# Layer 1 of a two-layer trunk: the loads of a recurrence unit in a task of their own, the exponential taken in place, and a shorter step of the recurrence's clock

## The chip, the cores and the metric

The kernel runs on one core of one Trainium2 chip. The metric is the device time of one execution in microseconds (us); lower is better. The times before are the median of three executions, 2402.3 us (2398.12 to 2408.5). One further execution was profiled.

## The reference, cut to what matters

A trunk of two layers works on x of 512 tokens by 2048 channels. Layer 0 is softmax attention with forget gates. Layer 1 is RWKV-7 time mixing, and the change lies there. Its heads have 64 channels each:

```python
w_log = -jax.nn.softplus(-(w0 + jnp.tanh(xw @ w1) @ w2)) - 0.5
decay = jnp.exp(-jnp.exp(w_log))
def step(S, inp):                       # one token, for each of 32 heads
    r_t, w_t, k_t, v_t, a_t, b_t = inp
    sa = einsum('bhvk,bhk->bhv', S, a_t)
    S = S * w_t + sa[..., None] * b_t + v_t[..., None] * k_t
    y_t = einsum('bhvk,bhk->bhv', S, r_t)
    return S, y_t
y = groupnorm(y) + sum(rh * kh * r_k) * vh
out = (y * silu(z)) @ w_out
```

## The kernel before, in words

**How the work is laid out.** Every large product (q, k, v, z, r and the two output projections) is a matrix of 16 by 16 blocks of 128 by 128. A block times 128 x 512 activations takes three TensorE matmuls, since weights and activations are split into a high and a low part (`mm3`, lines 253 to 258). These matmuls write the tiles `pj`. For every four blocks of weights there is one load of 256 KB (`raw`), one copy on ScalarE that makes the high part (`whi`) and one subtraction on VectorE that makes the low part (`wlo`).

**The recurrence.** Layer 1's recurrence is done in chunks of 64 tokens. There are four head groups of eight heads, and each has eight chunks, two to a unit: 16 units, numbered 0 to 15 here, and 32 chunks. For each unit `stage` (lines 1477 to 1527) loads three things with DMAs that SyncE (SP) issues: `rt` (256 KB), `bk` (four loads of 128 KB) and `prk` (256 KB, the running sum of the log decay, from the DRAM tensor `ipd`). Then ScalarE makes `eI`, the exponential of that sum; VectorE multiplies `rt` by `eI`, and GpSimd copies the chunk's total decay to `dec`. VectorE writes into `prk` the product of `rt`, a vector and `bk` in eight steps (tile `prk` again, lines 1499 to 1505). Then each chunk's loads `L`, `QP` and `SV` are issued, and a task `products` is started for each chunk. `products` makes the chunk's small matrices through two PSUM banks `S` (lines 1529 to 1567; ScalarE reads them into `L` and `GP`) and ends with the copy `tok`. `recur` (lines 1590 to 1644) carries the state `SV` from chunk to chunk in three steps: small matmuls into `x`, copies by VectorE into `xs` and `SV`, and again. `normed` normalizes a unit's output and stores it to `ypd`; `gated` loads it back (`yp`), multiplies by the gate (`z`), and from there the operands of the last projection are made (`gd`, `hp`, `hi`, `lo`).

**What sets the order.** All tasks are generators run by a small planner (`Flow`, lines 108 to 129). Its clock advances with the matmuls as they are issued, by 512/2400 us for a `pj` matmul. A task that yields d is resumed d planner microseconds later. `backbone` issues the `pj` matmuls one after another and lets due tasks put their instructions between them. So the order of each engine's instructions is fixed when the program is built; on the chip each engine works its own list in order and waits on semaphores for the others. SP's list is kept free for the scheduler to arrange within the dependencies.

**Numbers that matter here.** `STW` = 5 is the planner time between the load of `prk` and the exponential. `HOP` = 3.9 is the grid on which the recurrence's steps fall (`hop`, lines 1585 to 1588), three steps to a chunk. At most four chunks are staged and not yet consumed (`free["chunk"]`), and `rt`, `bk`, `prk` and `eI` have two buffers each.

Of the kernel before, what the change touches and what calls it, by code (L numbers as in the profile page):

```python
# [9 lines left out]
F = mybir.dt.float32  # L10
R = mybir.dt.float32r
AF = mybir.ActivationFunctionType
# [5 lines left out]
P = 128  # L18
# [6 lines left out]
C = 64  # L25
NCH = T // C
NJ, UC = 4, 2
# [104 lines left out]
def body(ctx, tc, a, out, dbg=None, stop=0):  # L132
# [1339 lines left out]

    HS = (slice(0, 64), slice(64, 128))
    OS = (slice(64, 128), slice(0, 64))
    QP, GP, svs, staged = [], [], {}, {}

    def stage(q, g, u):

        rt = q.tile([P, NJ, UC, C], F, tag="rt", name="rt", bufs=2)
        sp.dma_start(rt.rearrange("p j c t -> p j (c t)"), rTd[g][:, u])  # L1480
        bk = q.tile([P, NJ, UC, 2, C], F, tag="bk", name="bk", bufs=2)
        yield 1
        for i in range(2):
            for h in range(2):
                sp.dma_start(bk.rearrange("p j c i t -> p (j c) i t")[HS[h], :, i, :],
                             bkd[g][HS[h], u, i ^ h].rearrange("p j (c t) -> p (j c) t", c=UC))
            yield 0.6
        yield from take("prk")
        prk = q.tile([P, NJ, UC, C], F, tag="prk", name="prk", bufs=2)
        sp.dma_start(prk.rearrange("p j c t -> p j (c t)"), ipd[g][:, u])  # L1490
        yield STW
        eI = q.tile([P, NJ, UC, C], F, tag="eI", name="eI", bufs=2)
        act.activation(eI, prk, AF.Exp, scale=-EDEC)
        yield 1
        dec = q.tile([P, NJ, UC], F, tag="dec", name="dec", bufs=3)
        pool.tensor_copy(dec, eI[:, :, :, C - 1])
        dve.tensor_tensor(out=rt, in0=rt, in1=eI, op=OP.mult)
        yield 1
        for j in range(NJ):
            for h in range(2):  # L1500
                s = HS[h]
                dve.scalar_tensor_tensor(out=prk[s, j], in0=rt[s, j],
                                         scalar=vecs[s, V_RK, NJ * g + j:NJ * g + j + 1],
                                         in1=bk[s, j, :, 1 - h, :], op0=OP.mult, op1=OP.mult)
            yield 0.6
        while any(NJ * g + i not in vd for i in range(NJ)):
            yield 0.2
        for c in range(UC):
            yield from take("chunk")
            m = NCH * g + UC * u + c  # L1510
            L, SV = ([q.tile([P, NJ] + w, F, tag=f"{m}{h}", name=f"{m}{h}", bufs=4)
                      for h in range(2)] for m, w in (("L", [2, C]), ("SV", [C])))
# [12 lines left out]
            fl.start(fl.t + STW, products(q, m, c, L, SV, qp, bk, eI, dec))  # L1525
            yield 2
        fl.start(fl.t + 2, bonus(q, g, u, prk))

    def products(q, m, c, L, SV, qp, bk, eI, dec):

        gp = GP[m % 4]
        yield from hop()
        ns = yield from need2("S")
        gs = [bank("S") for _ in ns]
        for j in range(NJ):
            for h in range(2):
                s = HS[h]
                pe.matmul(gs[h][:, j * P:(j + 1) * P],
                          bk[s, j, c].rearrange("p a t -> p (a t)"),
                          L[h][s, j].rearrange("p a t -> p (a t)"), start=True, stop=True)  # L1540
        yield 0.9
        for h in range(2):
            s, t = HS[h], OS[h]
            g3 = gs[h].rearrange("p (j n) -> p j n", j=NJ)
            act.activation(L[h][t].rearrange("p j a t -> p j (a t)"), g3[t], AF.Copy)
            act.activation(gp[h][s], g3[s, :, C:], AF.Copy)
            read("S", ns[h])
            pool.affine_select(out=L[h][t], in_=L[h][t], pattern=[[0, NJ], [1, 2], [1, C]],
                               compare_op=OP.is_ge, fill=0.0, base=-1,
                               channel_multiplier=-1)  # L1550
            pool.affine_select(out=gp[h][s], in_=gp[h][s], pattern=[[0, NJ], [1, C]],
                               compare_op=OP.is_ge, fill=0.0, base=0, channel_multiplier=-1)
            yield 0.9
        pool.tensor_tensor(out=bk[:, :, c], in0=bk[:, :, c],
                           in1=eI[:, :, c, C - 1:C].unsqueeze(2).broadcast_to([P, NJ, 2, C]),
                           op=OP.mult)
        yield 4
        n = yield from need("S")
        tr = bank("S")
        for j in range(NJ):  # L1560
            pe.transpose(tr[:, j * P:(j + 1) * P], bk[:, j, c].rearrange("p a t -> p (a t)"),
                         ident)
        yield 0.6
        tok = q.tile([P, NJ, 2, C], F, tag="tok", name="tok", bufs=4)
        act.activation(tok.rearrange("p j h t -> p (j h t)"), tr, AF.Copy)
        read("S", n)
        staged[m] = SV, L, qp, gp, dec, tok

    def bonus(q, g, u, prk):
        vv = q.tile([P, T], F, tag="vv", name="vv", bufs=1)  # L1570
# [181 lines left out]

    STW = 5
    DG, DINV = (3,), 32
    HOP = 3.9
    INV, KEY = 54, 9.8

    def side(q):
        for j, o in enumerate(ks):
            fl.start(0, keep(j, o))  # L1760
        for k in range(KT):
            fl.start(fl.t, lora_k(q, k))
            yield 5.2
        while len(lb) < 4:
            yield 0.2
        yield 0.5
        pools.close()
        q = pools.enter_context(tc.tile_pool(name="uq", bufs=2, reuse_waits="tile"))
        for n in range(3):
            fl.start(fl.t, lora_w(q, 0, n))  # L1770
        rmask = q.tile([P, NCH, C], F, name="rmask", bufs=1)
        pool.memset(rmask, 1.0)
        pool.memset(rmask[:, :, 0:1], 0.0)
        rms.append(rmask)
        lora_act(q)
# [12 lines left out]
        eIs.append(kp.tile([P, NCH, C + 1], F, name="eI"))  # L1788
        for i in range(5):
            qts.append(kp.tile([P, NCH, C], F, name=f"qt{i}"))  # L1790
            for r in (32, 96):
                pool.memset(qts[i][r:r + 32, :, 0:32], 0.0)
        pool.memset(eIs[0][:, :, 0:1], 1.0)
        for j in range(KT):
            if "v" in dbg:
                print("keys", j, fl.t, len(ends))
            fl.start(fl.t, keys(kp, j))
            fl.start(fl.t + 5, mixz(kp, j))
            yield KEY
        while len(qd) < KT or len(premixed) < 3 * KT:  # L1800
            yield 0.2
        yield 3
        pools.close()
        rk = pools.enter_context(tc.tile_pool(name="rk", bufs=1, reuse_waits="tile"))
        for i in range(4):
            QP.append([rk.tile([P, NJ, C], F, name=f"QP{i}{h}") for h in range(2)])
            GP.append([rk.tile([P, NJ, C], F, name=f"GP{i}{h}") for h in range(2)])
            for h in range(2):
                pool.memset(QP[i][h][OS[h]], 0.0)
                pool.memset(GP[i][h][OS[h]], 0.0)  # L1810
        def stages():
            for n in range(NG * NU):
                g, u = divmod(n, NU)
                while any(NJ * g + i not in rd for i in range(NJ)):
                    yield 0.2
                yield from stage(rk, g, u)

        fl.start(fl.t, stages())
        fl.start(fl.t, recur(rk))

# [40 lines left out]
```

## Time and profile before

| | |
|---|---|
| median of three runs | 2402.3 us (2398.12 to 2408.5) |
| the profiled execution's own time | 2401.73 us |
| span from its first to its last instruction | 2399.9 us |
| TensorE (PE) busy | 2302.2 us, 96% |
| VectorE (DVE), ScalarE (ACT), GpSimd (POOL) busy | 1605.2, 1256.5, 694.4 us |
| layer 1's recurrence: first load of a unit to last `ypd` store issued | 1698.4 to 2197.7 us of the span |

A row of the timeline gives the start in us of the span, how long it took, the engine, the operation, what it wrote and read, and in square brackets how long the engine was idle before it and what ended that. SPq is the queue of SP, whose rows are issues of DMAs; the landing comes later. All instructions go through a helper on line 90, so they are told apart by their tiles. The row of an engine's waits names who waited, for whom, and gives the total, the count and the longest. In the table of windows the columns are the stretch and its length, then busy time and count for PE, PE's weight load, DVE, ACT and POOL, then the granted TensorE clock, the DMA engines' busy share and GB/s.

### The profile page before, as it was taken

The page shows a single profiled execution, that of the slowest core. Times are in us where ns is not written, and L with a number is a line of the kernel's source. Part 1 is how long each engine was busy: PE and PEld are TensorE (multiplying, and loading weights), DVE is VectorE, ACT ScalarE, POOL GpSimd, SP SyncE. Part 2 cuts the span into 40 slices and gives each one's busy share as a digit, 9 for nine tenths or more (in the row PEclk, how much of TensorE's full clock was granted, in tenths as well). Part 3 has the DMA queues.
Part 4 walks back from the last instruction along what each step waited for, and adds up shares of the span by engine and source line. Part 5 has one row for each costly group of instructions (what it writes and reads, how often), then busy time and mean ns, then how long its engine had stood idle before and what let it go on. Part 6 is the DMA issues. An engine that isn't in the chain of part 4 may idle for free. (4 is left out here: it accounts for less than half of the span.)

```text
span 2399.9 us, 39413 instructions
## 1 busy us (share of the span) xinstructions
PE 2302.2 (96%) x13626; PEld 1807.3 (75%) x13626; DVE 1605.2 (67%) x2850; ACT 1256.5 (52%) x2300; POOL 694.4 (29%) x1114
## 2 busy tenths in 40 slices
PE   6999999999999999998999898899999899999999
PEld 4787777877778778886777676677777677777787
DVE  6886778888888635336797567666476776755322
ACT  4435655555565545225646777763345556665221
POOL 0002333442424210110141208771245535450000
PEclk8999999999999999999999999899999999999999
DMA  8864466766666346445756999886867766544543
GB/s 307 328 227 156 128 211 217 222 213 213 205 224 220 114 161 225 142 141 157 223 179 198 308 263 277 256 252 187 233 187 195 219 174 194 167 132 154 161 137 97
DMA packets 388152, 480.23 MB, mean 200 GB/s; under 512 B 146032, under 2 KB 217840, under 8 KB 384112
## 3 DMA queue, kind: packets, MB, share of 16 engines
q1 hardware_dynamic: 386288, 475.08, 63.7%
q0 software_dynamic: 1664, 2.63, 0.3%
q8 instruction: 108, 1.77, 0.3%
q14 instruction: 92, 0.75, 0.1%
HBM read 381.63 MB, written 95.95 MB: 199 GB/s over the span
## 5 line engine op out<-in xcount | busy, mean ns | idle before, releaser
L90 PE MATMUL pj<-hi,whi 128*128 128x512 f32 x2416 | 987.4, 409 | 11.0 <-ACT hi L90 8.2
L90 PE MATMUL pj<-hi,wlo 128*128 128x512 f32 x2416 | 959.4, 397 | 10.1 <-DVE wlo L90 10.0
L90 PE MATMUL pj<-lo,whi 128*128 128x512 f32 x2416 | 959.9, 397 | 0.0
L90 DVE TENSOR_TENSOR wlo<-raw,whi 128x512 fp32r<-128x512 f32 (+2 forms) x628 | 473.4, 761 | 255.1 <-ACT whi L90 252.4
L90 ACT ACTIVATE whi<-raw 128x512 fp32r<-128x512 f32 (+2 forms) x628 | 393.9, 634 | 399.0 <-PE pj L90 215.1
L90 PEld LDWEIGHTS pj<-hi,whi 128*128 128x128 f32 x2416 | 459.5, 190 | 116.8 <-ACT hi L90 9.2
L90 PEld LDWEIGHTS pj<-lo,whi 128*128 128x128 f32 x2416 | 458.3, 190 | 108.4 <-DVE lo L90 0.7
L90 PEld LDWEIGHTS pj<-hi,wlo 128*128 128x128 f32 x2416 | 459.9, 190 | 105.2 <-DVE wlo L90 13.4
L90 DVE CUSTOM_DVE_ANT_0 wm<-wm,cb 128x1024 f32<-128x1024 f32 x128 | 155.8, 1217 | 0.3
L90 POOL TENSOR_SCALAR SV<-SV,dec 64x64 f32<-64x64 f32 x224 | 94.2, 442 | 103.9 <-DVE SV L90 69.7
L90 ACT ACTIVATE pr<-Sm,mx 128x128 f32<-128x128 f32 (+3 forms) x128 | 71.5, 559 | 76.8 <-POOL mx L90 76.3
L90 POOL TENSOR_SCALAR pr<-pr,rc 128x128 f32<-128x128 f32 (+3 forms) x128 | 100.8, 788 | 26.0 <-DVE rc L90 23.6
L90 POOL TENSOR_SCALAR mx<-mx 128x1 f32<-128x1 f32 x128 | 59.9, 468 | 143.2 <-DVE mx L90 98.0
L90 DVE CUSTOM_DVE_ANT_0 Sm<-S,cmask 128x128 f32<-128x128 f32 (+3 forms) x128 | 62.3, 487 | 42.5 <-PE S L90 41.8
L90 POOL TENSOR_TENSOR lt<-lane 128x30 f32<-128x30 f32 (+14 forms) x90 | 64.2, 713 | 86.4 <-DMA lane<-mld 79.6
L90 POOL TENSOR_TENSOR bk<-bk,eI 128x512 f32<-128x512 f32 x32 | 36.6, 1142 | 110.3 <-PE S L90 64.0
L90 POOL TENSOR_TENSOR lane<-lane,lt 128x30 f32<-128x30 f32 (+14 forms) x90 | 64.0, 711 | 7.0
L90 PE MATMUL S<-k,q 128*128 128x128 f32 (+7 forms) x256 | 61.9, 323 | 0.0
L90 POOL TENSOR_TENSOR acc<-acc,sq 128x512 f32<-128x512 f32 x14 | 18.1, 1296 | 149.4 <-ACT sq L90 128.2
L90 ACT ACTIVATE pT<-tr 128x512 f32<-128x512 f32 x64 | 31.0, 485 | 54.4 <-PE tr L90 54.4
L90 DVE SCALAR_TENSOR_TENSOR hp<-pj,gate,hp 128x512 f32<-128x512 f32 x16 | 12.0, 751 | 68.0 <-PE pj L90 68.0
L90 PE MATMUL tr<-ident,pr 128*128 128x128 f32 x320 | 56.0, 273 | 1.5 <-DVE pT L90 1.3
(325 smaller groups left out, 3284.0 us busy)
## 6 DMA issues: line engine op xcount, KB each, us to landing
wm<-in_wmodT SPq DMA_DIRECT2D x132, 512.0 KB, 4.4
raw<-in_wz SPq DMA_DIRECT2D x128, 256.0 KB, 3.7
raw<-in_wo SPq DMA_DIRECT2D x128, 256.0 KB, 3.6
raw<-in_wv SPq DMA_DIRECT2D x124, 256.0 KB, 3.9
wm<-in_wmodT SPq DMA_DIRECT2D x30, 1024.0 KB, 6.4
raw<-in_wk SPq DMA_DIRECT2D x96, 256.0 KB, 3.7
raw<-in_wr SPq DMA_DIRECT2D x64, 256.0 KB, 5.0
raw<-in_wq SPq DMA_DIRECT2D x56, 256.0 KB, 3.5
```

Of the source, the lines that this page charges most:

```text
L90: self.last = f(*a, **k)
```

## The change

The loads move out of `stage` into a new task, `arrive`. A second generator, `arrivals`, runs it for the units in order, as soon as the group's `rt` is ready (as before) and, for units 2 and on, once the last chunk of the unit before the one before has been made (`made`, set by `products` after `tok`). `stages` starts 9 planner us later than before and waits until a unit's loads have all been issued (`got`). The running sum is no longer loaded into `prk` but into `eI`, and the exponential is taken in place; `prk` only receives the product. The load of the sum moves from behind the loads of `bk` to before them, and `bk`'s four loads are a planner microsecond apart each. The fixed `yield STW` ahead of the exponential is gone (`STW` stays in use ahead of `products`). `HOP` is 3.75 in place of 3.9.

```diff
-    def stage(q, g, u):
+    def arrive(q, g, u, got):
         rt = q.tile([P, NJ, UC, C], F, tag="rt", name="rt", bufs=2)
         sp.dma_start(rt.rearrange("p j c t -> p j (c t)"), rTd[g][:, u])
+        yield 1
+        eI = q.tile([P, NJ, UC, C], F, tag="eI", name="eI", bufs=2)
+        sp.dma_start(eI.rearrange("p j c t -> p j (c t)"), ipd[g][:, u])
+        yield 1
         bk = q.tile([P, NJ, UC, 2, C], F, tag="bk", name="bk", bufs=2)
-        yield 1
         for i in range(2):
             for h in range(2):
                 sp.dma_start(bk.rearrange("p j c i t -> p (j c) i t")[HS[h], :, i, :],
                              bkd[g][HS[h], u, i ^ h].rearrange("p j (c t) -> p (j c) t", c=UC))
-            yield 0.6
+                yield 1
+        got[NU * g + u] = rt, eI, bk
+
+    def stage(q, g, u, rt, eI, bk):
         yield from take("prk")
         prk = q.tile([P, NJ, UC, C], F, tag="prk", name="prk", bufs=2)
-        sp.dma_start(prk.rearrange("p j c t -> p j (c t)"), ipd[g][:, u])
-        yield STW
-        eI = q.tile([P, NJ, UC, C], F, tag="eI", name="eI", bufs=2)
-        act.activation(eI, prk, AF.Exp, scale=-EDEC)
+        act.activation(eI, eI, AF.Exp, scale=-EDEC)
...
         staged[m] = SV, L, qp, gp, dec, tok
+        made.add(m)
...
-    HOP = 3.9
+    HOP = 3.75
...
+        got = {}
+
+        def arrivals():
             for n in range(NG * NU):
                 g, u = divmod(n, NU)
-                while any(NJ * g + i not in rd for i in range(NJ)):
+                while any(NJ * g + i not in rd for i in range(NJ)) or \
+                        n > 1 and UC * (n - 1) - 1 not in made:
                     yield 0.2
-                yield from stage(rk, g, u)
+                yield from arrive(rk, g, u, got)
 
+        def stages():
+            yield 9
+            for n in range(NG * NU):
+                while n not in got:
+                    yield 0.2
+                yield from stage(rk, *divmod(n, NU), *got.pop(n))
+
+        fl.start(fl.t, arrivals())
         fl.start(fl.t, stages())
```

What the change makes of the order of instructions shows at three places. First SP's list at unit 10 (third head group), from the load of `rt` on. The number behind a name tells one buffer's use from the next; `x2` are two like rows. Before:

```order
L90 DMA rt_20570<-rTd_125 128x512
L90 DMA SV0_20528<-vtd_127 64x256
L90 DMA SV1_20529<-vtd_127 64x256
L90 DMA bk_20572<-bkd_117 64x8x64 x2
L90 DMA vv_20616<-vvd_126 128x512
L90 DMA bk_20572<-bkd_117 64x8x64 x2
L90 DMA yp_20626<-ypd_128 128x4x128
L90 DMA prk_20633<-ipd_122 128x512
L90 DMA raw_20635<-in_wz1 128x512
```

And the same place now:

```order
L90 DMA rt_20473<-rTd_125 128x512
L90 DMA eI_20481<-ipd_122 128x512
L90 DMA bk_20486<-bkd_117 64x8x64 x2
L90 DMA L0_20513<-atd_116 64x4x64
L90 DMA QP30_17180<-qtd_118 64x4x64
L90 DMA SV0_20515<-vtd_127 64x256
L90 DMA L1_20514<-atd_116 64x4x64
L90 DMA QP31_17181<-qtd_118 64x4x64
L90 DMA SV1_20516<-vtd_127 64x256
L90 DMA bk_20486<-bkd_117 64x8x64
L90 DMA raw_20543<-in_wz1 128x512
L90 DMA bk_20486<-bkd_117 64x8x64
```

The running sum's load stands right behind `rt`'s, where eight other loads stood between them, and the last two loads of `bk` now stand behind six loads of another unit's chunk.

Next DVE's list at the same unit, from the last weight part ahead of the unit on. `rt<-rt,eI` is the first use of the exponential, `prk<-rt,vecs,bk` the first use of `bk`, and `SV`, `xs` and `x` are the recurrence. Before:

```order
L90 TENSOR_TENSOR wlo_20701<-raw_20635,whi_20700 128x512
L90 TENSOR_TENSOR rt_20570<-rt_20570,eI_20703 128x512
L90 SCALAR_TENSOR_TENSOR prk_20633<-rt_20570,vecs_63,bk_20572 64x128 x2
L90 TENSOR_TENSOR mlo_20746<-prk_20296,mhi_20745 128x512
L90 SCALAR_TENSOR_TENSOR prk_20633<-rt_20570,vecs_63,bk_20572 64x128 x4
L90 COPY xs_20784<-x_20775 128x256
L90 SCALAR_TENSOR_TENSOR prk_20633<-rt_20570,vecs_63,bk_20572 64x128 x2
```

And now:

```order
L90 TENSOR_TENSOR mlo_20549<-ys_20537,mhi_20548 128x512
L90 TENSOR_TENSOR rt_20473<-rt_20473,eI_20481 128x512
L90 SCALAR_TENSOR_TENSOR prk_20588<-rt_20473,vecs_63,bk_20486 64x128 x4
L90 COPY SV0_19950<-x_20559 64x256
L90 COPY SV1_19951<-x_20559 64x256
L90 SCALAR_TENSOR_TENSOR prk_20588<-rt_20473,vecs_63,bk_20486 64x128 x4
L90 TENSOR_TENSOR mlo_20636<-sq_20603,mhi_20635 128x512
```

The uses of the exponential and of `bk` follow each other as before; two copies of the recurrence's state now stand between the two halves of `bk`'s use.

Last DVE's list near the end of layer 1, where `z<-z,yp` applies the gate to tiles 12 and 13, `wlo` are weights, and `lo<-hp,hi` are operands of the last projection. Before:

```order
L90 TENSOR_TENSOR lo_23527<-hp_23452,hi_23526 128x512
L90 TENSOR_TENSOR z_23381<-z_23381,yp_23471 128x512
L90 TENSOR_TENSOR z_23272<-z_23272,yp_23473 128x512
L90 TENSOR_TENSOR lo_23541<-hp_23468,hi_23540 128x512
L90 TENSOR_TENSOR lo_23558<-hp_23485,hi_23557 128x512
L90 TENSOR_TENSOR wlo_23555<-raw_23496,whi_23554 128x512
L90 TENSOR_TENSOR lo_23578<-hp_23502,hi_23577 128x512
L90 TENSOR_TENSOR wlo_23570<-raw_23508,whi_23569 128x512
```

And now:

```order
L90 TENSOR_TENSOR z_23310<-z_23310,yp_23352 128x512
L90 TENSOR_TENSOR wlo_23400<-raw_23363,whi_23399 128x512
L90 TENSOR_TENSOR wlo_23432<-raw_23381,whi_23431 128x512
L90 TENSOR_TENSOR lo_23435<-hp_23406,hi_23434 128x512
L90 TENSOR_TENSOR lo_23453<-hp_23413,hi_23452 128x512
L90 TENSOR_TENSOR z_23402<-z_23402,yp_23404 128x512
L90 TENSOR_TENSOR lo_23469<-hp_23415,hi_23468 128x512
L90 TENSOR_TENSOR wlo_23466<-raw_23408,whi_23465 128x512
```

The two gatings stood one behind the other, seven operands deep into the last projection's list; now the first stands ahead of the first of these operands, and the second two operands behind it.

More of the change, by code (lines that the diff above doesn't have):

```diff
@@ L1474, in body @@
     OS = (slice(64, 128), slice(0, 64))
-    QP, GP, svs, staged = [], [], {}, {}
-    def stage(q, g, u):
+    QP, GP, svs, staged, made = [], [], {}, {}, set()
+    def arrive(q, g, u, got):
         rt = q.tile([P, NJ, UC, C], F, tag="rt", name="rt", bufs=2)
         sp.dma_start(rt.rearrange("p j c t -> p j (c t)"), rTd[g][:, u])
+        yield 1
+        eI = q.tile([P, NJ, UC, C], F, tag="eI", name="eI", bufs=2)
+        sp.dma_start(eI.rearrange("p j c t -> p j (c t)"), ipd[g][:, u])
+        yield 1
         bk = q.tile([P, NJ, UC, 2, C], F, tag="bk", name="bk", bufs=2)
-        yield 1
         for i in range(2):
@@ L1810, in side @@
                 pool.memset(GP[i][h][OS[h]], 0.0)
-        def stages():
+        got = {}
+        def arrivals():
             for n in range(NG * NU):
                 g, u = divmod(n, NU)
-                while any(NJ * g + i not in rd for i in range(NJ)):
+                while any(NJ * g + i not in rd for i in range(NJ)) or \
+                        n > 1 and UC * (n - 1) - 1 not in made:
                     yield 0.2
-                yield from stage(rk, g, u)
+                yield from arrive(rk, g, u, got)
[6 more added lines that the diff above has]
+        fl.start(fl.t, arrivals())
         fl.start(fl.t, stages())
```

## The prediction

> **What bounds the kernel now.** The page comes first, for what is busy and for how long.
>
> ```profile
> span 2399.9 us, 39413 instructions
> PE 2302.2 (96%) x13626; PEld 1807.3 (75%) x13626; DVE 1605.2 (67%) x2850; ACT 1256.5 (52%) x2300; POOL 694.4 (29%) x1114
> ```
>
> PE is the bound, and the change neither adds nor removes a matmul. So time can only come from the stretches in which PE stands still or has half its clock, and only behind the first instruction that moves, the loads of unit 0 at 1698 us. The windows of 100 us from there say how much there is (the first column after the length is PE's busy time; the granted clock stands behind POOL's count).
>
> ```profile
> 1700.00:1800.00 100.00, 96.26 (x804) 76.14 (x804) 64.84 (x133) 43.14 (x80) 44.91 (x93) 0.98 0.77 205
> 1800.00:1900.00 100.00, 98.56 (x1000) 77.40 (x998) 76.92 (x169) 53.71 (x100) 51.23 (x94) 1.00 0.71 197
> 1900.00:2000.00 100.00, 89.86 (x892) 69.22 (x893) 71.46 (x146) 57.22 (x100) 43.78 (x88) 0.97 0.69 192
> 2000.00:2100.00 100.00, 98.86 (x970) 77.49 (x969) 70.00 (x157) 65.55 (x106) 47.67 (x90) 1.00 0.64 181
> 2100.00:2200.00 100.00, 99.44 (x880) 78.39 (x877) 55.65 (x122) 59.52 (x96) 32.08 (x61) 1.00 0.38 117
> 2200.00:2300.00 100.00, 97.01 (x414) 77.23 (x413) 38.64 (x60) 30.39 (x49) 0.00 (x0) 1.00 0.58 176
> ```
>
> PE's idle time is 3.74 + 1.44 + 10.14 + 1.14 + 0.56 + 2.99 = 20.0 us: 0.8% of the kernel, and half of it in one window. That is the ceiling of any gain, but for the clock. PE's waits in this stretch and the timeline say what the idle time is made of.
>
> ```profile
> PE S L90 <- ACT GP L90: 9.7, 5, 5.3
> PE S L90 <- ACT mhi L90: 3.5, 1, 3.5
> PE pj L90 <- DVE wlo L90: 2.9, 3, 1.5
> ...
> 1907.04 0.42 SPq L90 DMA_DIRECT2D rt<-rTd  x1
> 1911.91 0.89 SPq L90 DMA_DIRECT2D prk<-ipd  x1
> 1917.31 0.63 ACT L90 ACTIVATE eI<-prk 128x512 f32<-128x512 f32 x1 [4.09 <-DMA prk<-ipd]
> 1918.96 0.38 ACT L90 ACTIVATE GP<-S 64x256 f32<-64x256 f32 x1
> 1919.39 0.79 PE L90 MATMUL S<-mhi,blkr 128*128 128x512 f32 x1 [5.28 <-ACT GP L90]
> ```
>
> This is unit 8, the largest stall. SP issued the load of the running sum 4.87 us behind that of `rt`, since `bk`'s loads and others stood between. ACT reached the exponential first and waited 4.09 us for the load. The reads of the PSUM banks (`L`, `GP`) stood behind it in ACT's list, PE needed such a bank, and so PE stood still for 5.28 us. The same chain shows once more in small, at unit 5:
>
> ```profile
> 1830.10 0.63 ACT L90 ACTIVATE eI<-prk 128x512 f32<-128x512 f32 x1 [1.60 <-DMA prk<-ipd]
> 1831.67 0.50 PE L90 MATMUL S<-mhi,blkr 128*128 128x512 f32 x1 [1.00 <-ACT GP L90]
> ```
>
> Two of 16 units paid on PE. The large stall also cost clock: the windows of 20 us show a granted clock of 0.93 behind it.
>
> ```profile
> 1900.00:1920.00 20.00, 12.80 (x142) 9.64 (x142) 13.02 (x22) 11.62 (x22) 13.60 (x29) 0.90 0.90 257
> 1920.00:1940.00 20.00, 19.03 (x185) 14.72 (x184) 18.80 (x41) 10.93 (x20) 6.32 (x12) 0.93 0.61 161
> 1940.00:1960.00 20.00, 19.56 (x178) 15.24 (x179) 15.74 (x35) 9.40 (x17) 6.89 (x17) 1.00 0.56 149
> ```
>
> In 1920 to 1940 that is 20 x 0.07 = 1.4 us of matmul time lost. The Trainium skill ("TensorE: Matmul & The Clock Gate", the section on what is actually happening) has the clock halved once PE was idle for a window of some 3.4 us, and restored after a busy window as long: by it the price would be an estimated 1.7 us. By that rule the sum below would be 0.3 us larger; the row decides.
>
> The other big stall, at 1737, has another cause: ACT waited for a weight load. The clock behind it was 0.95, 20 x 0.05 = 1 us.
>
> ```profile
> 1735.81 0.63 ACT L90 ACTIVATE whi<-raw 128x512 fp32r<-128x512 f32 x1 [3.08 <-DMA raw<-in_wv]
> 1737.01 0.49 PE L90 MATMUL S<-mhi,blkr 128*128 128x512 f32 x1 [3.46 <-ACT mhi L90]
> ...
> 1740.00:1760.00 20.00, 20.00 (x200) 16.05 (x197) 11.01 (x24) 8.79 (x17) 9.21 (x17) 0.95 0.72 195
> ```
>
> **The exponential's load comes sooner.** By the planner's yields nothing is gained: from the load of `eI` to `got` there are still five yields of 1, as STW was 5. The rest of "one unit ahead" is small, because `arrivals` must wait until the unit before last is made. What does gain is SP's list. Between the loads of `rt` and of the sum stood 4 to 8 other issues at units 0 to 10 before; now at most 4 do, and mostly none or one. For unit 8, with its gap of 4.87 us, one is left. What a load takes from issue to landing, and what an issue takes of SP, stands in the rows of the tiles `prk` and `bk` (the latter in 1690 to 2200):
>
> ```profile
> L90 SPq DMA_DIRECT2D prk<-ipd x16: 326/680/1747, 1702.2 to 2089.8; - x16
> DMA to landing us min/median/max: 2.6/4.7/5.9
> ...
> L90 SPq DMA_DIRECT2D bk<-bkd x64: 573/626/1296, 1698.9 to 2103.9; - x64
> DMA to landing us min/median/max: 2.6/4.4/6.3
> ```
>
> Planner time is shorter than the chip's. A row near the end of the chain of waits gives PE's pace without disturbance:
>
> ```profile
> 2226.59 169.46 PE pj L90 x728
> ```
>
> A `pj` matmul takes 169.46 / 728 = 0.233 us where the planner books 0.213, a ratio of 1.09. Five planner microseconds are 5.5 us, more than the median landing of 4.7 and less than the longest, 5.9: at most 0.4 us of wait is left. So I take off unit 8's 5.28 + 1.4 and unit 5's 1.00: **-7.7 us**. Bounds: 0, if the loads slip as before, and -7.7.
>
> **The shorter HOP and the end of the recurrence.** In PE's list the first chunk's `x` stands behind 5304 `pj` matmuls (5295 before), the last chunk's behind 6267 (6321 before). The recurrence ends 54 x 0.233 = 12.6 us of filler earlier. That by itself is no time, as PE's filler only changes places. It pays where the end is late today, at the last projection:
>
> ```profile
> 2208.99 0.69 DVE L90 TENSOR_TENSOR z<-z,yp 128x512 f32<-128x512 f32 x1 [3.85 <-DMA yp<-ypd]
> 2211.55 0.50 PE L90 MATMUL pj<-hi,wlo 128*128 128x512 f32 x1 [0.77 <-DVE wlo L90]
> 2218.96 0.50 PE L90 MATMUL pj<-hi,wlo 128*128 128x512 f32 x1 [1.55 <-DVE wlo L90]
> 2225.24 0.69 DVE L90 TENSOR_TENSOR z<-z,yp 128x512 f32<-128x512 f32 x1 [2.54 <-DMA yp<-ypd]
> 2226.59 0.50 PE L90 MATMUL pj<-hi,wlo 128*128 128x512 f32 x1 [0.57 <-DVE wlo L90]
> ```
>
> Tiles 12 and 13 waited in DVE's list, with weights behind them; their operands came late. Both gatings now stand some 12 us earlier against the filler, and 0.77 + 1.55 go: **-2.3 us** (bounds 0 and -2.9). Tiles 14 and 15 stand where they stood, since they follow their own matmuls; the 0.57 stays. A tighter recurrence costs nothing on PE, I think: its dependent steps in PE's list are about as far apart at the least as before, 2.4 us of other matmuls counted at the pace above.
>
> **`bk` comes later, and this costs.** Before, the last load of `bk` was issued 0.6 + 5 + 1 + 1 = 7.6 planner us ahead of its first use; now at least 1 + 1 + 1 = 3, or 3.3 us on the chip, where landing takes 4.4 in the median. That alone is 1.1 us of wait on DVE for each unit. SP's list is worse: in ten of the 16 units the last load of `bk` stands 10 to 15 issues behind that of `eI` (12.8 in the mean, the others' chunk loads between), where at units 0 to 12 it stood ahead of the sum's load. Twelve or thirteen issues are 12.8 x 0.626 = 8.0 us, and with 4.4 to land 12.4; the first use is due 7 planner us behind `eI`'s load at the least, 7.6 us. The wait is then up to 4.8 us. I take half, 2.4 us at ten units, 24 us of DVE, since stages that wait for a chunk leave more lead and SP often runs ahead.
>
> What PE pays of it: a wait of DVE of 3.85 us let PE stand for 0.77 (rows above), a fifth; ACT's wait of 4.09 cost 5.28, 1.3 times. Behind `bk`'s use stand weights, covered by the parts made ahead, and the state copies of the recurrence, which PE wants only a step later. I take the fifth, as the row of the same engine: **+4.8 us**. Bounds: 0, and 10 x 4.8 x 1.3 = +62, which I hold for far out. The Trainium skill ("DMA: Bandwidth & Descriptors", the rules for kernel authors) advises to issue a DMA early and wait for it late; by that rule the edit to `bk` is the wrong way round. The page's fit for the GpSimd path (anatomy of one DMA, 2.0 us and the bytes at 436 GB/s) would have 128 KB land in an estimated 2.3 us, and the sum without this cost; the trace's 4.4 decides.
>
> **The rest.** The exponential in place, `prk` without a load and the wait for `made` add no instruction that computes. SP may wait for a buffer: `eI` and `bk` are now loaded soon after the unit before last is made. Weights queue behind that on SP, three buffers deep. I count nothing for it. The stalls of 3.46 at 1737 and the remainder I leave as they are: other orders make other stalls of this size.
>
> **Sum.** -7.7 - 2.3 + 4.8 = -5.2. The profiled execution took 2401.73 us, span and 1.8 us around it; that gives 2396.5. The median of the runs is 0.6 higher: **2397 us**.
>
> **Rivals.** Half a per cent, 12 us, is about what a measurement of this kernel can tell from no change.
>
> - *`bk` waits land on PE.* With 48 us of DVE waits (ten times 4.8) and the state copies `SV` right behind them in DVE's list, PE pays more than a fifth. For it: a whole step of the recurrence is only 3.75 planner us, 4.1 us, and copies held for 4.8 exceed it. Against it: most steps have slack from DVE's own speed. It decides from a share of 22 / 48 = 0.46 on; at 0.6 it gives 2402.3 - 10 + 29 = 2421.
> - *Even pace.* In PE's list the two `products` of a unit stood mostly 9 to 15 `pj` apart; from unit 3 on they stand 24 to 39 apart. If this also clears half of the remaining 20.0 - 5.28 - 1.00 - 2.32 = 11.4 us of stalls, and `bk` costs nothing: 2402.3 - 10.0 - 5.7 = 2386.6. With all of it and the clock lost behind the stall at 1737, some 1 us, 2380 is the floor.
> - *It isn't ahead.* If the lead of 5.5 us is eaten by SP, ACT waits as before, and only the end gains: 2402.3 - 2.3 = 2400.
>
> **Chances.** Forecast 0.45, not ahead 0.15 (both within 0.5%), even pace 0.28, `bk` on PE 0.12. So faster by over 0.5% 0.28, within 0.60, slower 0.12. The range reaches to most of the even pace and part way into the `bk` case: 2384 to 2410.
>
> **What would show it.** Right: no ACT wait of over 1 us ahead of `eI`, no stall of PE over 3.4 us behind it and a clock of 1.00 there; DVE waits for `bk` ahead of `prk` in several units; of the three `wlo` stalls at the end one left. Wrong: PE's idle time behind 1698 us falling under 9 us, or rising over 25 with `x` or `S` waiting for DVE's `SV` or `mlo` behind `prk`.

## The result, and the profile after

The changed kernel takes 2426.3 us (median of four runs, 2422.03 to 2430.04) beside 2400.3 for the kernel before (2398.12 to 2408.5, now with a fourth run; three gave 2402.3): a ratio of 1.0102, 95% interval 1.0082 to 1.0122. By the medians it is 26 us slower, and the forecast of 2397 with its range of 2384 to 2410 is wrong in sign and size.

The profiled execution of the changed kernel took 2428.13 us. Its page has the same matmuls, and more busy time on VectorE (DVE) and GpSimd (POOL):

```profile
span 2426.4 us, 39363 instructions
PE 2310.3 (95%) x13626; PEld 1809.1 (75%) x13626; DVE 1621.2 (67%) x2850; ACT 1257.1 (52%) x2301; POOL 705.1 (29%) x1114
```

The windows of 100 us over the recurrence, in the columns of the prediction's table, show where the time went:

```profile
1700.00:1800.00 100.00, 94.44 (x770) 74.30 (x769) 64.53 (x126) 41.58 (x78) 46.59 (x93) 0.95 0.77 202
1800.00:1900.00 100.00, 92.75 (x895) 71.20 (x894) 69.40 (x146) 47.59 (x90) 42.78 (x88) 0.95 0.64 173
1900.00:2000.00 100.00, 87.61 (x872) 67.39 (x872) 81.39 (x161) 55.46 (x98) 47.36 (x80) 0.97 0.65 176
2000.00:2100.00 100.00, 94.51 (x930) 72.69 (x929) 67.57 (x141) 64.80 (x104) 51.61 (x90) 0.98 0.65 185
2100.00:2200.00 100.00, 95.74 (x949) 74.26 (x946) 61.15 (x126) 54.80 (x89) 39.48 (x74) 1.00 0.40 122
2200.00:2300.00 100.00, 100.00 (x431) 80.50 (x430) 42.19 (x70) 39.46 (x65) 0.00 (x0) 1.00 0.55 171
```

PE's idle time is 5.56 + 7.25 + 12.39 + 5.49 + 4.26 + 0 = 34.95 us, where it was 20.0: 15 us more. The shares below full clock (the last column but two) add up to 5 + 5 + 3 + 2 = 15 in a hundred of 100 us, where they were 2 + 3 = 5: some 10 us more. The two make 25 of the 26.5 us by which the span grew. PE's waits between 1690 and 2300 us name what it stood for:

```profile
PE S L90 <- DVE mlo L90: 23.8, 16, 5.2
PE S L90 <- DMA raw<-in_wv: 3.3, 1, 3.3
...
PE S L90 <- ACT GP L90: 2.0, 2, 1.8
```

Before, the waits for `mlo` were 1.8 us and those for `GP` 9.7. `mlo` is the low part of what `means` sums with two matmuls: ScalarE (ACT) makes the high part `mhi`, DVE subtracts it, and 1.8 planner us after the subtraction is issued the matmuls stand in PE's list (line 1103 of the kernel before, `yield 1.8`). The recurrence calls `means` three times a unit: in `bonus` over `prk`, and in `normed` over `ys` and `sq`. The largest stall, in the timeline, first ACT and PE, then DVE:

```profile
1898.71 0.62 ACT L90 ACTIVATE mhi<-prk 128x512 fp32r<-128x512 f32 x1
1901.49 0.47 PE L90 MATMUL S<-mhi,blkr 128*128 128x512 f32 x1
1907.16 0.79 PE L90 MATMUL S<-mlo,blkr 128*128 128x512 f32 x1 [5.20 <-DVE mlo L90]
...
1897.82 0.74 DVE L90 SCALAR_TENSOR_TENSOR prk<-rt,vecs,bk 64x128 f32<-64x128 f32 x2
1898.59 2.15 DVE L90 SCALAR_TENSOR_TENSOR dc<-dc,vecs,sq 128x128 f32<-128x128 f32 x4
1900.66 2.42 DVE L90 SCALAR_TENSOR_TENSOR dc<-dc,vecs,bv 128x128 f32<-128x128 f32 x4
1903.01 0.70 DVE L90 SCALAR_TENSOR_TENSOR prk<-rt,vecs,bk 64x128 f32<-64x128 f32 x2
1903.74 0.69 DVE L90 TENSOR_TENSOR lo<-hp,hi 128x512 fp32r<-128x512 f32 x1
1904.35 0.68 DVE L90 TENSOR_TENSOR wlo<-raw,whi 128x512 fp32r<-128x512 f32 x1
1904.95 1.43 DVE L90 SCALAR_TENSOR_TENSOR prk<-rt,vecs,bk 64x128 f32<-64x128 f32 x4
1906.41 0.69 DVE L90 TENSOR_TENSOR mlo<-prk,mhi 128x512 fp32r<-128x512 f32 x1
```

`mhi` had been made at 1899.3, and DVE didn't wait for anything: it worked off its list. Ahead of `mlo` stood eight steps of one unit's normalization (`dc`) and the eight `prk` steps of unit 7, the next unit. In the kernel before, DVE's timeline has the `mlo` of the same place, with two of unit 7's `prk` steps ahead of it and the `dc` steps 3.5 us behind it:

```profile
1887.89 0.75 DVE L90 SCALAR_TENSOR_TENSOR prk<-rt,vecs,bk 64x128 f32<-64x128 f32 x2
1888.67 0.70 DVE L90 TENSOR_TENSOR mlo<-prk,mhi 128x512 fp32r<-128x512 f32 x1
1889.29 1.49 DVE L90 SCALAR_TENSOR_TENSOR prk<-rt,vecs,bk 64x128 f32<-64x128 f32 x4
...
1892.16 1.14 DVE L90 SCALAR_TENSOR_TENSOR dc<-dc,vecs,sq 128x128 f32<-128x128 f32 x4
```

It is not one place alone. In the changed kernel's trace the bonus's `mlo` stands behind six or more `dc` steps at eight of the 16 units and starts 3.3 to 7.1 us after its `mhi` was made; before, it stood behind four of them at one unit (2.6 us). The `mlo` over `sq` stands behind `prk` steps at eight units, before at none. Of the 23.8 us of PE's waits, 13.7 are the bonus's, 8.4 those over `sq` and 1.7 those over `ys`.

What the prediction had named first did come. The only wait left ahead of an exponential, and all that DVE waits for `bk` ahead of `prk`, are these rows of the timeline and of DVE's waits:

```profile
1749.45 0.63 ACT L90 ACTIVATE eI<-eI 128x512 f32<-128x512 f32 x1 [0.17 <-DMA eI<-ipd]
...
DVE prk L90 <- DMA bk<-bkd: 1.2, 2, 0.8
```

One of the two waits for `bk` is at unit 8. The rows are SP's issues of the third and the fourth load, and DVE's first use:

```profile
1922.79 0.60 SPq L90 DMA_DIRECT2D bk<-bkd  x1
1924.57 0.58 SPq L90 DMA_DIRECT2D bk<-bkd  x1
1925.57 1.99 DVE L90 SCALAR_TENSOR_TENSOR prk<-rt,vecs,bk 64x128 f32<-64x128 f32 x4 [0.49 <-DMA bk<-bkd]
```

In the trace the third load lands at 1925.48 and the fourth at 1928.27, when four of the eight steps are done. The steps read `bk[s, j, :, 1 - h, :]`, and that is what the second and the third load bring; the fourth they don't need.

### The profile page after: what moved, and what is told of

It is laid out like the page before. It is cut to its first block, busy times and chain, and to the rows that moved or that the text cites. A ratio compares the mean times of both kernels' runs of the same rounds, so it can differ in the third digit from the quotient of the medians.

```text
span 2426.4 us, 39363 instructions
## 1 busy us (share of the span) xinstructions
PE 2310.3 (95%) x13626; PEld 1809.1 (75%) x13626; DVE 1621.2 (67%) x2850; ACT 1257.1 (52%) x2301; POOL 705.1 (29%) x1114
## 5 line engine op out<-in xcount | busy, mean ns | idle before, releaser
L90 POOL TENSOR_SCALAR pr<-pr,rc 128x128 f32<-128x128 f32 (+3 forms) x128 | 101.2, 791 | 25.8 <-DVE rc L90 23.6
```

The costliest lines, as they stand in the source:

```text
L90: self.last = f(*a, **k)
```

## The experiments

Three theories stood at first. **A**: the unit's DVE work now falls together with the normalization's, and the sums' low parts queue behind both, more than 1.8 planner us allow. **B**: the shorter step is too tight for the recurrence. **C**: `bk` is loaded too late. After the second set came **D**: the constants of the kernel before are a fitted set, and any shift of the unit's stages against the recurrence makes some meetings of the engines late, each time others.

All results, each beside the kernel before on the same chip. The sets of runs were taken on different chips, on which the kernel before took 2398.4 to 2402.5 us; so kernels are compared by their ratios. The waits are PE's, in us, between 1690 and 2300 us of the profiled run, which can lie some us off the median (for e18 2442.1 beside 2433.6): for `mlo`; of `pj` (for `z` or `wlo`, in the tail); and the largest others ("issue" is time in which PE waited for nothing that the profile shows).

| kernel | median, us | ratio (95%) | mlo | pj | others |
|---|---|---|---|---|---|
| before | 2400.3 | 1 | 1.8 | 2.9 | GP 9.7, mhi 3.5 |
| changed | 2426.3 | 1.0102 (1.0082 to 1.0122) | 23.8 | 0 | raw 3.3, mhi 2.3 |
| e1 changed, HOP 3.9 | 2415.8 | 1.0072 (1.0052 to 1.0092) | 7.0 | 6.1 | GP 8.3, bv 4.0 |
| e2 before, HOP 3.75 | 2411.4 | 1.0057 (1.0036 to 1.0077) | 2.7 | 0.2 | GP 5.5, dec 3.8 |
| e3 changed, exponential late | 2412.8 | 1.0064 (1.0044 to 1.0084) | 15.0 | 0.2 | sq 3.3, vf 3.1 |
| e4 changed, allowance 4 | 2402.7 | 1.0018 (1.0008 to 1.0027) | 0 | 1.2 | GP 9.5, vf 2.8 |
| e5 changed, `dc` late | 2415.5 | 1.0065 (1.0050 to 1.0080) | 9.8 | 0 | GP 5.6, bv 4.9 |
| e6 before, HOP 3.85 | 2407.5 | 1.0035 (1.0025 to 1.0046) | 2.7 | 1.8 | issue 6.5, xs 3.2 |
| e7 changed, HOP 3.9, exponential late | 2422.9 | 1.0090 (1.0075 to 1.0105) | 10.1 | 11.2 | xs 5.2, mhi 3.3 |
| e8 before, allowance 4 | 2403.9 | 1.0012 (1.0002 to 1.0023) | 0 | 7.2 | GP 4.2, vf 3.6 |
| e9 before, STW 4.5 | 2412.0 | 1.0050 (1.0034 to 1.0066) | 4.3 | 2.9 | xs 6.3, vf 5.1 |
| e10 before, HOP 3.95 | 2414.7 | 1.0058 (1.0043 to 1.0073) | 3.4 | 5.7 | GP 7.7, mhi 3.2 |
| e11 changed, HOP 3.9, allowance 4 | 2405.7 | 1.0019 (1.0007 to 1.0031) | 0.6 | 9.9 | dc 3.3, GP 3.0 |
| e12 changed, exponential late, allowance 4 | 2409.5 | 1.0041 (1.0027 to 1.0056) | 0.2 | 1.5 | vf 7.3, bv 3.7 |
| e13 before, STW 4.5, allowance 4 | 2406.3 | 1.0024 (1.0012 to 1.0037) | 0 | 7.1 | GP 8.1, vf 6.0 |
| e14 before, HOP 3.95, allowance 4 | 2407.0 | 1.0029 (1.0017 to 1.0040) | 0 | 6.3 | GP 5.2, vf 3.6 |
| e15a changed, HOP 3.85, allowance 4 | 2403.6 | 1.0010 (0.9998 to 1.0023) | 0 | 6.0 | dc 4.6, GP 3.9 |
| e15b changed, HOP 3.8, allowance 4 | 2406.1 | 1.0025 (1.0010 to 1.0041) | 0 | 3.6 | vf 4.4, dc 4.2 |
| e17 changed, allowance 3 | 2401.5 | 1.0006 (0.9993 to 1.0018) | 0 | 0 | SV 3.9, GP 3.7 |
| e18 changed, allowance 5 | 2433.6 | 1.0137 (1.0106 to 1.0169) | 0 | 2.5 | GP 23.4, SV 6.0 |

### One part at a time

e1 leaves the loads' task and undoes the step; e2 does the step alone, on the kernel before; e6 does a third of the step.

```diff
 e1, on the changed kernel
-    HOP = 3.75
+    HOP = 3.9
 e2, on the kernel before (e6: 3.85)
-    HOP = 3.9
+    HOP = 3.75
```

> The change with the recurrence's step back at 3.9. Theory A (the unit's work on VectorE now falls together with the normalization's and the sums' low parts queue behind it; the step is no cause): stays slow, 2415 to 2430 us, PE's waits for mlo behind 1690 us 15 us or more. Theory B (the shorter step is too tight for the recurrence): back to 2400 or less, mlo waits under 6 us. Theory C (bk is loaded too late): stays slow too, as C does not touch the step.

> The kernel before with the shorter step alone. A: the unit's work keeps its distance from the normalization's, since the fixed wait ahead of the exponential stays; 2395 to 2406 us, PE's mlo waits under 8 us. B: 2420 us or more. C: as before, 2400.

> The kernel before with the step at 3.85, a third of the way to 3.75, which cost 13 us. A: in VectorE's list most bonus sums again stand ahead of the dc steps, as at 3.9; 2395 to 2403 us. B (the loss grows with tightness): a third, 2401 to 2406.

Each part alone makes the kernel slower: the loads' task by 0.72%, the step by 0.57%, a third of the step by 0.35%. The sum, 1.3%, is not far from the 1.02% of both. None of the three came as a theory had it: e1 has the time that A gave and less than half of its waits, e2 lies between A and B, e6 above both. The waits for `mlo`, 7.0 and 2.7, don't add up to 23.8; most of e2's loss is in short waits of other kinds. PE's waits of e2:

```profile
PE S L90 <- ACT GP L90: 5.5, 5, 2.9
PE S L90 <- POOL dec L90: 3.8, 1, 3.8
PE S L90 <- ACT mhi L90: 3.8, 2, 2.8
...
PE S L90 <- DVE mlo L90: 2.7, 3, 1.5
```

So the step costs on PE by itself, and hardly through the sums.

### The allowance, and the two kinds of DVE work pulled apart

e4 gives the recurrence's three sums 4 planner us in place of 1.8. e3 delays the exponential, and with it `prk`, as before the change; e5 delays the `dc` steps.

```diff
 e4, on the changed kernel (e8 on the kernel before; e17: 3, e18: 5)
-    def means(q, w, x, th, tl):
+    def means(q, w, x, th, tl, wait=1.8):
...
-        yield 1.8
+        yield wait
...
+        bo, n = yield from means(q, blkr, prk.rearrange("p j c t -> p (j c t)"), "mh", "ml", 4)
+        d, n = yield from means(q, centerr, ys, "mh", "ml", 4)
+        vr, n = yield from means(q, blkr, sq, "mh", "ml", 4)
 e3, on the changed kernel
+        yield STW
         act.activation(eI, eI, AF.Exp, scale=-EDEC)
 e5, on the changed kernel, ahead of the dc steps
-        yield 2
+        yield 6
```

> The change with the fixed wait of 5 planner us put back ahead of the exponential; the loads stay in their own task and so come 5 earlier against their use than in the change. A: the unit's work moves off the normalization's; 2395 to 2408 us, mlo waits under 10 us. B: no help, 2420 to 2430. C: bk has 8 planner us of lead again, so also fast; the DMA waits ahead of prk, 1.2 us in the change, then tell A from C: C needs them to be large in the change, which they are not.

> The change with the planner's allowance between a sum's low part on VectorE and its matmul raised from 1.8 to 4 in the recurrence's three sums; nothing else moves by hand. A: the backlog stays, but PE meets it later; mlo waits fall from 23.8 to under 8 us, 2396 to 2410 us. B and C: PE's loss has another source, the time stays within 8 us of 2426.

> The change with the normalization's eight closing steps on VectorE (dc) put off by 4 planner us. Theory A (low parts of the sums queue on VectorE behind bursts of another task): the bonus sum's low part now stands ahead of these steps, and its five waits of 3.08, 5.20, 2.06, 1.03 and 2.10 us go; those of the other sum, behind the prk steps, stay. Mlo waits 23.8 to about 10 us, 2404 to 2414 us. Theory B (a tighter recurrence) and theory C (bk loaded late) see no gain: 2420 to 2430.

e4 comes as A has it: the ratio falls from 1.0102 to 1.0018, which is some 20 of the 24 us. From 1900 to 2000 us PE idles 5.6 us, where the changed kernel had 12.4; its waits have no `mlo`, and as much for `GP` as the kernel before had:

```profile
1900.00:2000.00 100.00, 94.45 (x951) 73.84 (x950) 85.30 (x165) 62.60 (x111) 53.15 (x94) 0.98 0.71 197
...
PE S L90 <- ACT GP L90: 9.5, 4, 3.4
```

Pulling the DVE work apart helps in part: `mlo` falls to 15.0 (e3) and 9.8 (e5), and the ratio to 1.0064 and 1.0065, some 9 us each. e5's waits are as A has them and its time is 1.5 us above A's range; e3 missed A's range in both. By sums, each delay takes away the waits behind the work that it moves:

| PE's waits for `mlo`, us | bonus | over `sq` |
|---|---|---|
| changed | 13.7 | 8.4 |
| e3, `prk` steps late | 13.9 | 1.1 |
| e5, `dc` steps late | 2.8 | 6.6 |

So the work ahead in DVE's list is what these waits are made of. The time follows only in part, as both leave or bring other waits.

### Does theory A explain all of it?

e7 does the loads' task alone, with the step and the exponential's delay of before; e8 gives the kernel before the allowance.

```diff
 e7, on the changed kernel
-    HOP = 3.75
+    HOP = 3.9
...
+        yield STW
         act.activation(eI, eI, AF.Exp, scale=-EDEC)
```

> The change with both the step of 3.9 and the fixed wait ahead of the exponential, so that only the loads' own task, their order and the exponential in place are left. A: the unit's work on VectorE keeps the distance that it had before; 2396 to 2406 us. C (bk behind the exponential's load, and issues of other chunks between): still 2410 or more.

> The kernel before with the allowance of 4 between a sum's low part and its matmul. A: before had only 1.8 us of such waits, so nothing to win there: 2395 to 2405. If the allowance is good in itself (it also gives ScalarE time), it falls to 2393 or less.

e8 came as A has it: the kernel before has no such waits to lose, and gains nothing. e7 felled A as the whole story. With the step and the delay of before it takes 2422.9, no faster than e1 by the ratios (1.0090 and 1.0072, and the intervals overlap), and its waits are spread:

```profile
PE S L90 <- DVE mlo L90: 10.1, 9, 1.9
PE pj L90 <- ACT z L90: 6.9, 1, 6.9
PE x L90 <- DVE xs L90: 5.2, 4, 2.0
PE pj L90 <- DVE wlo L90: 4.3, 1, 4.3
```

The time is one that C has too (2410 or more), but C doesn't explain it: `bk` isn't among these waits, nor among DVE's in e7.

### The constants of the kernel before

This led to theory D. e9 and e10 move no load and no line; each changes one constant of the kernel before.

```diff
 e9
-    STW = 5
+    STW = 4.5
 e10
-    HOP = 3.9
+    HOP = 3.95
```

> The kernel before with STW = 4.5 for 5: only a constant that delays the exponential behind the unit's loads and the products behind the chunk's loads, by half a planned microsecond less; no load, buffer or line is moved. Theory A (the unit's DVE work and the normalization's fall together, the sums' low parts queue behind them, and only that makes the changed kernel slow) gives 2398 to 2402, with under 3 us of PE's waits for mlo. Theory D (the constants of the kernel before were fitted together: nothing in the plan books the other engines' time, so any shift of the unit's stages against the recurrence lets some meetings come late, each time others) gives 2404 to 2412, from stalls of several tiles, no one of them over 8 us in all.

> The kernel before with HOP = 3.95 for 3.9: the recurrence's step is longer, where 3.85 and 3.75 were shorter and cost 8 and 11 to 13 us. A theory by which a shorter step is too tight for the chain on the chip (B) gives no loss from a longer one but the later end, 2398 to 2404. Theory D (fitted constants) gives 2403 to 2412, as for a shorter one, with stalls of other tiles than the kernel before has.

Half a planner microsecond less ahead of the exponential and the products costs 0.50%; a step longer by 0.05 costs 0.58%, as much as a step shorter by 0.15. That is D's side (e10 2.7 us above its range); A had no loss there and B hardly one. The waits of e9 are of many kinds:

```profile
PE x L90 <- DVE xs L90: 6.3, 4, 2.2
PE S L90 <- DVE vf L90: 5.1, 3, 2.4
...
PE S L90 <- DVE mlo L90: 4.3, 7, 1.0
```

### The allowance on shifted kernels

e11 to e15b are kernels above with e4's allowance of 4:

```diff
 e11: e1 with 4; e12: e3 with 4; e13: e9 with 4; e14: e10 with 4
 e15a and e15b, e4 with
-    HOP = 3.75
+    HOP = 3.85
 and
+    HOP = 3.8
```

> The changed kernel with HOP = 3.9 and 4 instead of 1.8 planned microseconds between the issue of the sums' low part and its matmul, for the recurrence's three sums. With HOP = 3.9 alone it took 2415.8, 7.0 us of its PE waits for mlo and 5.8 in the tail for the gates' z. Theory A: the mlo waits go (under 1 us) and what the clock lost with them, 2402 to 2409, and the tail's wait for z stays, since the later end of the recurrence causes it. Theory D: other meetings take the place of those, 2409 to 2418.

> The changed kernel (HOP = 3.75) with both remedies that helped: the exponential late again by STW (alone 2412.8) and 4 planned microseconds for the sums' low part (alone 2402.7). Theory A: the first only moved the unit's DVE work away from the sums, which the second makes harmless, so the two together give no more than the second alone, 2399 to 2405, mlo under 1 us. Theory C (the unit's input comes too late where the exponential is early) gives under 2398. Theory D gives anything from 2402 to 2412 with stalls of tiles other than mlo.

> The kernel before with STW = 4.5 (alone 2412.0, with 4.3 us of waits for mlo) and 4 for 1.8 planned microseconds ahead of the sums' low part. Theory A in its wide form (the short allowance is what makes every shift dear) gives 2400 to 2406. Theory D (a shift makes other meetings late, each time others, and the allowance helps only where mlo is the one) takes away the 4.3 and little more, and may bring as much: 2406 to 2414.

> The kernel before with HOP = 3.95 (alone 2414.7, with 3.4 us of waits for mlo, 7.7 for GP and 5.7 for wlo in the tail) and the allowance of 4. Theory A in its wide form gives 2400 to 2407. Theory D gives 2408 to 2416, with the waits for GP and the tail's wait still there.

> The changed kernel with HOP = 3.85 and the allowance of 4. With the allowance it took 2402.7 at a step of 3.75 (9.5 us of waits for GP) and 2405.7 at 3.9 (8.1 in the tail for z). Theory A: 2398 to 2405, mlo under 1 us, the tail's wait under 4. Theory D: no order in the step, 2402 to 2412.

> The changed kernel with HOP = 3.8 and the allowance of 4. Theory A: 2397 to 2404, mlo under 1 us, no wait over 2 us in the tail. Theory D: no order in the step, 2402 to 2412.

In ratios, the allowance takes e1 from 1.0072 to 1.0019, e3 from 1.0064 to 1.0041, e9 from 1.0050 to 1.0024 and e10 from 1.0058 to 1.0029. Without it the shifted kernels lie between 1.0035 and 1.0102, with it between 1.0010 and 1.0041. So it takes off a third to three quarters, in e9 and e10 more than their 4.3 and 3.4 us of waits for `mlo`; for e3 and e12 the two intervals overlap. What is left is spread over `GP`, `vf` and `dc`, without an order of the step that the intervals show. The ranges don't decide between A in its wide form and D: e11 and e14 came in A's and below D's, e12 and e15b in D's and above A's, e13 at their border and e15a in both (with 6.0 us in the tail, where A had under 4). The tail follows the step where the allowance is 4: `pj` waits of 9.9 us at 3.9, 6.0 at 3.85, 3.6 at 3.8, 1.2 at 3.75. e12 missed A's range: with the allowance there, the late exponential costs some 5 us more than the early one of e4 (1.0041 beside 1.0018; the two intervals just touch).

### The size of the allowance

> The changed kernel with 3 instead of 1.8 planned microseconds ahead of the sums' low part. Theory A: each wait for mlo becomes 1.2 us shorter; of the 23.6 us of such waits in the changed kernel (5.2, 3.1, 2.1, 2.1, 2.0, 1.9, 1.7, 1.7, 1.4, 1.0 and five under 0.4) some 10.4 stay, and the time comes down by about 13, to 2408 to 2417, between the 2426.3 at 1.8 and the 2402.7 at 4. Theory D (any new order, good or bad by chance) gives 2402 to 2424, with mlo anywhere between 0 and 15 and no link of the time to it.

> The changed kernel with 5 instead of 1.8 planned microseconds ahead of the sums' low part. Theory A: nothing more to win than at 4, since no wait for mlo was left there, 2400 to 2406; the longer bonus and normalization may hold buffers longer. Theory D gives 2402 to 2412, and stalls of tiles that 4 did not show.

Both of A's numbers fell, and D's at 5 with them. At 3 no wait for `mlo` was left, where 10.4 us were expected, and the time is that of the kernel before; at 5 the whole loss is back (its interval overlaps the changed kernel's). A stall isn't shortened by what its allowance grows: the planner lays all later work anew. The traces show what that did here. A normalization holds two of the three sums, so its `dc` steps move back by twice the added allowance: with 3, 4 or 5 no bonus `mlo` stands behind four or more `dc` steps any more, as at eight units of the changed kernel. The `mlo` over `sq` still stands behind `prk` steps, in e17 at ten units and up to 3.9 us behind its `mhi`; PE has no wait left there. What 5 costs, the trace of e18 shows. ACT's waits, then SP's queue, ACT and PE around the largest stall:

```profile
ACT ys L90 <- DMA ypd<-dc: 61.5, 15, 7.9
...
2153.43 0.33 SPq L90 DMA_DIRECT2D ypd<-dc  x1
2155.62 0.60 ACT L90 ACTIVATE ys<-y 128x512 f32<-128x512 f32 x1 [6.31 <-DMA ypd<-dc]
2156.86 0.38 ACT L90 ACTIVATE GP<-S 64x256 f32<-64x256 f32 x1
2157.29 0.79 PE L90 MATMUL S<-mhi,blkr 128*128 128x512 f32 x1 [5.29 <-ACT GP L90]
```

`ys` and `dc` have the same tag in a pool with one buffer for each. By its yields a normalization takes at the least 8.5 planner us and twice the allowance until `dc` is stored: 18.5 at 5, or 20.2 us at the pace of 1.09. In e18's trace it is 25.8 us in the median from `ys` to the store's issue (18.3 in the changed kernel), and the store lands 2.0 to 3.3 us later. A unit has six steps of 3.75, or 24.5 us. So the store lands after the next unit's `ys` is due, at all 15 units that have one before them; ACT then stands, the reads of the PSUM banks stand behind it in its list, and PE waits for a bank. That is 61.5 us of ACT. Of PE's 23.4 us for `GP`, some 16 come within 3 us of the end of such a stand of ACT; the 3.3 us at 1734 and the 3.7 at 1779 lie ahead of the first one. In the kernel before the same row of ACT's waits says 10.6 us, in the changed kernel 1.8, with the allowance of 4 16.4. The order in time is shown; that a second buffer would cure it was not tried.

No version beats the kernel before. The best of the changed ones, e17 and e15a, can't be told from it.

## Why the prediction was wrong

- **The exponential's load**: right. The waits ahead of the exponential went from 7.5 us to 0.2, those for `GP` from 9.7 to 2.0. The lead came out longer than reckoned: the exponential starts 12.1 us (median) behind the issue of its load, where 7.0 were measured before and five planner us, 5.5 us, were counted on; so "one unit ahead" was not small. The gain is not the same in each order: e4, too, has no wait ahead of an exponential, and 9.5 us for `GP` from other causes. Given the allowance, the early exponential is worth some 5 us (e4 against e12).
- **The end of the recurrence**: right, and a little more: PE doesn't stand at all from 2200 to 2300 us, 2.99 us less, where 2.3 were forecast. The table's `pj` column shows the step as its cause: with the same loads and the same allowance, the shorter step has the smaller wait in all rows but one (e14 beside e8).
- **"`bk` comes later, and this costs"**: wrong, +4.8 forecast. DVE waited for `bk` 1.2 us in all, not 24. Two premises of the sum failed. It went by the landing of the last load, which the steps don't read (the rows of unit 8 above). And it set the first use 7.6 us behind the issue of `eI`'s load, the least that the yields allow; the trace has 9.3 to 25.1 us, 14.6 in the median. The third load landed ahead of the first use at all 16 units, by 0.1 to 11 us; at two of them DVE stood until it landed.
- **"A tighter recurrence costs nothing on PE, I think"**: failed. The step alone costs 13 to 14 us (e2), a third of it 8 (e6). I had looked at the distances of the recurrence's own steps in PE's list, where the cost lies in the tasks around them.
- **"Other orders make other stalls of this size"**: the step that failed worst. I took the stalls of the kernel before as what any order has, and the sum has no term for new ones. Four shifts by a constant alone, e2, e6, e9 and e10, cost 0.35 to 0.58%. The two parts of the change are two such shifts, and together they put the unit's `prk` and the `dc` steps in front of the sums, for 23.8 us of waits and part of 10 us of clock.
- **The rival on the slow side** had nearly the time, 2421, but by luck: it had DVE waiting for `bk` and the state copies `SV` held behind it, where DVE was full and the sums' `mlo` was held. That a full DVE list could hold PE was among none of the rivals, so a chance of 0.12 for "slower" was too small. The sign I gave for being wrong, idle time over 25 us with `S` waiting for `mlo` behind `prk`, is what the trace shows.

Shown is that the waits for `mlo` come from the `dc` and `prk` steps ahead in DVE's list (e3 and e5 each take away their part), that with an allowance of 3 or 4 these waits and nearly the whole loss are gone, and that each of the four shifts of `HOP` or `STW` tried on the kernel before is slower (`STW` was moved one way only). As each such edit also lays the later order anew, how much of the loss in time is these waits and how much the rest of the new order isn't separated: e3 and e5 take away 9 and 14 us of waits for some 9 us of time each. Open is also which meeting comes late for a given shift, and why.

## What to carry to other kernels

Where a planner books only one engine's time, its fixed yields are distances that hold for one order: before forecasting a shift as free, look for the waits it allows least (here 1.8 us for a subtraction in a queue that can hold 8 us of work) and ask what else now stands ahead in that in-order queue. A kernel's remaining stalls can be a lower end and not a typical draw, as they were here for `HOP` and `STW`; a constant moved by a hair is a cheap test of that, and belongs beside any change of order. And an allowance had two ends here: 1.8 was paid in waits, 5 in buffers held. It also moves the work that waits behind it, so its effect is read from the new order and not from the old stalls.

## What the runs showed of the hardware

**Short stalls can cost clock.** Windows of 4 us behind the stall of 2.02 us that ends at 1806.59 in the changed kernel, the only idle time in them:

```profile
1804.00:1808.00 4.00, 1.98 (x9) 1.37 (x7) 3.73 (x10) 0.86 (x2) 0.00 (x0) 0.82 0.82 265
1808.00:1812.00 4.00, 4.00 (x42) 3.00 (x41) 1.52 (x4) 2.26 (x5) 0.95 (x4) 0.75 0.11 24
...
1960.00:1980.00 20.00, 17.94 (x203) 14.09 (x202) 13.40 (x30) 8.50 (x17) 5.78 (x9) 1.00 0.56 148
```

That is 4 x 0.18 + 4 x 0.25 = 1.7 us of clock; in the trace's record of the clock it is half from 1806.60 to 1810.01, for 3.41 us. The last row holds a stall of 2.06 us that cost none. The Trainium skill ("TensorE: Matmul & The Clock Gate", the section on what is actually happening) has the clock fall after an idle window of some 3.4 us. By the Trainium skill's window at half clock the price is an estimated 1.7 us, and the 1.7 us of these rows agree with it. That 2.02 us of idling can be enough does not agree.

**DVE's steps grow beside GpSimd.** Mean ns of the `dc` and `prk` groups from 1690 to 2300 us, changed kernel, then before:

```profile
L90 DVE SCALAR_TENSOR_TENSOR prk<-rt,vecs,bk 64x128 f32<-64x128 f32 x128 | 49.7, 388 | 3.1 <-DMA bk<-bkd 1.2
L90 DVE SCALAR_TENSOR_TENSOR dc<-dc,vecs,sq 128x128 f32<-128x128 f32 x64 | 24.4, 439 | 5.3 <-ACT sq L90 5.1
...
L90 DVE SCALAR_TENSOR_TENSOR prk<-rt,vecs,bk 64x128 f32<-64x128 f32 x128 | 47.4, 371 | 1.7
L90 DVE SCALAR_TENSOR_TENSOR dc<-dc,vecs,sq 128x128 f32<-128x128 f32 x64 | 19.1, 361 | 0.9 <-ACT sq L90 0.7
```

Sorted by single instructions of the trace, 84 of the 128 `dc` steps overlap a GpSimd instruction in the changed kernel and take 470 ns in the mean, the other 44 take 342; before, 22 overlap (493) and 106 don't (347). The Trainium skill ("SBUF — State Buffer", the section on who interferes with whom) says that such a DVE step with two SBUF inputs and a GpSimd instruction that reads SBUF block each other for a whole instruction; the trace agrees: the last of the four `dc` steps that begin at 1898.59 takes 1.22 us, from 1899.52 on, and beside it GpSimd runs one product that reads SBUF, from 1899.55 to 1900.60. So the shift of the stages made the queue ahead of `mlo` not only fuller but slower: the four `dc` steps at 1898.59 took 2.15 us, those at 1892.16 before 1.14.
